# MLP up projection: GpSimd's subtractions, sums and low parts given to VectorE

## The chip, the core and the metric

The kernel runs on one core of one Trainium2 chip. The metric is the device time of one execution in microseconds. A core has five engines that work side by side, each through its own queue in order: TensorE (PE in the profile, with PEld for its weight loads), VectorE (DVE), ScalarE (ACT), GpSimd (POOL) and SyncE (SP), which here issues the DMA transfers.

## What is computed

A bidirectional encoder of two layers over 1024 tokens of width 1024, in float32. Layer 0 mixes tokens by attention, layer 1 by a gated delta rule, and each layer ends with the same gated MLP, of which this case changes the first half:

```python
D_MODEL = 1024; SEQ = 1024; D_FF = 2816; FFN_CONV = 3

def conv_ffn(h, w_up, conv_w, conv_b, w_down):
    u = depthwise_conv_centred(h @ w_up, conv_w, conv_b)
    a, b = jnp.split(u, 2, axis=-1)
    return (jax.nn.silu(a) * b) @ w_down

for i in range(DEPTH):
    y = rmsnorm(h, norm_mix[i])
    h = h + mixer(i, y)          # attention or gated delta rule, with its out projection
    h = h + conv_ffn(rmsnorm(h, norm_ffn[i]), ffn_w_up[i], ffn_conv_w[i], ffn_conv_b[i], ffn_w_down[i])
return rmsnorm(h, norm_final)
```

## The kernel before

**Split operands.** A float32 matrix is written as a high part and a low part. `split` (L108 to L110) has ScalarE cast x to the high part (L109), and another engine subtract that from x for the low part (L110): VectorE, unless the caller names an engine. `dense` (L126, its matmul is L134) then multiplies high by high, high by low and low by high, so that one 128x128 block of weights against 512 tokens takes three matmuls.

**Seven products for eight.** The up projection works on `f` from 0 to 21, each f being 128 columns of a and 128 of b. The tokens form two halves of 512 and the inner width two halves of 512, and a scheme of Strassen's kind computes the 2x2 block product with seven products p1 to p7 of 12 matmuls each, 84 in an f. TensorE takes them in the order p1, p2, p6, p5, p7, p3, p4. The weight operands are the four loaded blocks a11 to a22 and four sums `s` of them (L982, in `operands`); the token operands are named "11", "21", "t1" to "t4" and "22", and are made once in each layer by `tokens` (L893). In the trace the operands t1, t2, t3 have tiles t10h to t33l (k from 0 to 3, h high, l low), and "t4" and "22" lie in tiles called base.

**The transition.** `tokens` makes these operands while the out projection of the mixer still runs and the first f starts. The tokens come in three parts: 0:512, 512:768, 768:1024. For each part VectorE and GpSimd work out the scale 1/rms: VectorE takes mean and epsilon (L152), GpSimd the power (L153), TensorE spreads the result over the lanes (L166), and VectorE multiplies it into h (L190). Then come differences of h (L903) and their splits. Within `tokens` every third difference or low part is GpSimd's, by a counter. `start` computes p1 and p2 of f 0 and 1 before the last part is scaled; the other products of these two f wait for the last part's operands.

**The steady loop.** In each f from 2 on, VectorE makes low parts (L110) of the weight operands into tiles wl, of which three are held; two of the sums s; the first sum ua (L964), which adds p2 in tile mm to p1 and frees the accumulator that p5 of the same f writes; two further adds (L1002); four steps of the width-3 convolution (L1033 and L1035, for ua and then ub, after ScalarE has begun each at L1032); and the product with the gate (L1039). GpSimd makes the low parts of p6 and p4 and the first and third of the sums s. At each odd f, `take` of the down projection (L1057) makes four differences of the gated activations of this f and the one before (L1061, GpSimd, one of them in place in the even f's tile) and stores each by a DMA on SyncE's queue (L1060).

**The start of the down projection.** Behind the stores of the last pair, SyncE's queue holds the loads of stored activations (L1088, into raw) and of down weights (L1095).

The order of each engine's queue is fixed when the program is built, by priorities: code under `ahead(n)` is moved forward of what is written before it.

Of the kernel before, what the change touches and what calls it, by code (L numbers as in the profile page):

```python
# [13 lines left out]
ALU = mybir.AluOpType  # L14
# [862 lines left out]
class UpProjection:  # L877
# [15 lines left out]
    def tokens(self, gain):  # L893

        t, nc, h = self.t, self.nc, self.t.h
        n = [0]

        def engine():
            n[0] += 1
            return nc.vector if n[0] % 3 else nc.gpsimd  # L900

        def sub(x, z, out):
            engine().tensor_tensor(out=out, in0=x, in1=z, op=ALU.subtract)  # L903

        def put(name, k, xs, x):
            hi, lo = self.b[name][k]
            t.split(x, hi[:, xs], lo[:, xs], engine())

        with t.ahead(1):
            acc = t.big()  # L910
            bc = t.scales(HALVES[0], *(acc[:, b] for b in HALVES))
        for k in range(KT):
            x = h[k][:, HALVES[0]]
            t.scaled(x, x, gain[:, k:k + 1], bc)
            put("11" if k < 4 else "21", k % 4, slice(0, H2), x)
        ys = []
        for part, cs in enumerate(PARTS[1:]):
            xs = slice(cs.start - H2, cs.stop - H2)
            y = [[h[k][:, xs], h[k][:, cs]] for k in range(KT)]
            ys.append((xs, y))  # L920
            acc = t.bank() if part else t.big()
            with t.ahead(2):
                bc = t.scales(cs, acc[:, :2 * P], acc[:, H2 - 2 * P:H2] if part else acc[:, H2:H2 + 2 * P])
            if part == 1:
                with t.ahead(1):
                    self.start(2)
            for k in range(4):
                t.scaled(y[k][1], y[k][1], gain[:, k:k + 1], bc)
                sub(y[k][1], y[k][0], y[k][0])
                put("t1", k, xs, y[k][0])  # L930
            for k in range(4):
                t.scaled(y[k + 4][1], y[k + 4][1], gain[:, k + 4:k + 5], bc)
                sub(y[k + 4][1], y[k][0], y[k][0])
                put("t2", k, xs, y[k][0])
        for xs, y in ys:
            for k in range(4):
                sub(y[k + 4][1], y[k][1], y[k][1])
                put("t3", k, xs, y[k][1])
            for k in range(4):
                sub(y[k + 4][0], y[k][0], y[k + 4][0])  # L940
                put("t4", k, xs, y[k + 4][0])
                put("22", k, xs, y[k + 4][1])
# [23 lines left out]
    def operands(self, f):  # L966
        nc, raw = self.nc, []
        slot = lambda n: self.up.tile([P, H2], F32, name=n, bufs=2 if n[0] == "a" else 3)
        if f < 2:
            free = [self.gp.tile([P, H2], F32, name=n) for n in (3 - f) * ("gh", "gl")]  # L970
            free = iter(free if f else free + [self.rp.tile([P, H2], F32, name="raw") for _ in range(2)])
            slot = lambda n, up=slot: next(free, None) or up(n)
        for r in range(2):
            for k in range(2):
                x = slot(f"a{r}{k}")
                nc.sync.dma_start(out=x, in_=self.src(f, r, k).rearrange("p k n -> p (k n)"))
                raw.append(x)
        a11, a12, a21, a22 = raw
        s = [slot("s") for _ in range(4)]
        for i, (x, z, op, e) in enumerate(((a21, a22, ALU.add, nc.gpsimd), (s[0], a11, ALU.subtract, nc.vector),  # L980
                                           (a11, a21, ALU.subtract, nc.gpsimd), (a12, s[1], ALU.subtract, nc.vector))):
            e.tensor_tensor(out=s[i], in0=x, in1=z, op=op)  # L982
        return {"p1": (a11, "11"), "p2": (a12, "21"), "p5": (s[0], "t1"), "p6": (s[1], "t2"), "p7": (s[2], "t3"),
                "p4": (a22, "t4"), "p3": (s[3], "22")}

    def product(self, acc, ops, name, onto=False, early=0):

        x, col = ops[name]
        hi, lo = self.t.pair(self.t.wp, "w", H2)
        with self.t.ahead(early):  # L990
            self.t.split(x, hi, lo, self.nc.gpsimd if name in ("p6", "p4") else self.nc.vector)
        w = [(hi[:, k * P:(k + 1) * P], lo[:, k * P:(k + 1) * P]) for k in range(4)]
        self.t.dense(acc, w, self.b[col], [slice(0, H2)], onto=onto)

# [50 lines left out]
class DownProjection:  # L1045
# [11 lines left out]
    def take(self, f, g, pool):  # L1057

        nc = self.nc
        put = lambda n, x: nc.sync.dma_start(out=self.gd[n][f // 2], in_=x)  # L1060
        sub = lambda out, x, z: nc.gpsimd.tensor_tensor(out=out, in0=x, in1=z, op=ALU.subtract)  # L1061
        g0, g1 = (g[:, hs] for hs in HALVES)
        if f % 2 == 0:
            put("11", g0)
            self.even = g0, g1
            return
        b11, b12 = self.even
        put("21", g0)
        put("22", g1)
        t3 = pool.tile([P, H2], F32, name="t3", bufs=1)  # L1070
        sub(b11, b12, b11)
        put("t1", b11)
        sub(t3, g1, b12)
        put("t3", t3)
        sub(b12, g1, b11)
        put("t2", b12)
        sub(g0, g0, b12)
        put("t4", g0)
# [19 lines left out]
    def run(self):  # L1098
# [45 lines left out]
        a = [x[:, hs] for x in (t.big(), t.big()) for hs in HALVES]  # L1144
        b = [t.bank() for _ in range(4)]
        acc11 = product("11", w1, a, ys=lambda p: self.ready[p] if p < G_FIRST else self.tokens("11", p))
        residuals(range(4), 0)
        for m, acc in acc11:
            add(h(m, 0), acc, h(m, 0))
        a12 = [x[:, hs] for x in [t.base(i, F32) for i in range(2, 8)] for hs in HALVES][:NP]  # L1150
        for m, acc in product("21", lambda p: weights(self.load(a12[p], 0, 1, p)), b):
            read = add(h(m, 0), acc, h(m, 0))
            done(m, 0, m == 0)
# [10 lines left out]
        for m, acc in product("t1", w5, b, after=read):  # L1164
            add(h(4 + m, 1), acc, h(4 + m, 1))
# [230 lines left out]
```

## Time and profile before

| what | value |
|---|---|
| median of three runs | 3466.25 us (3457.93 to 3467.89) |
| the profiled execution: its time | 3468.96 us |
| the profiled execution: its span | 3467.2 us |
| mean granted TensorE clock | 0.976 of full speed |
| TensorE matmul busy | 3266.1 us, 94% |
| VectorE busy | 2474.7 us, 71% |
| ScalarE busy | 1730.5 us, 50% |
| GpSimd busy | 922.6 us, 27% |

The span runs from the first to the last instruction that the profiler saw; the profiled execution's own time is 1.8 us longer. A busy share is a mean over stages that have different limits, so for this change the stages count one by one: in layer 0 the transition lies at about 623 to 696 us, the steady loop at 696 to 1090 us and the start of the down projection right behind it; in layer 1 the same three lie at about 2769 to 2842, 2842 to 3222 and 3222 to 3255 us. In the timeline view a row gives start and duration of an instruction, and in brackets how long its engine sat idle before it and what ended that. "x4" in a timeline row are four instructions told as one.

### The profile page before, as it was taken

Reading aid. Unit: us, or ns where it says so; the run is one execution under the profiler, and the core shown is the slowest. Engines: PE = TensorE matmul, PEld = TensorE weight load, DVE = VectorE, ACT = ScalarE, POOL = GpSimd, SP = SyncE. Lnnn points to the kernel's source line nnn. Section 1 sums busy time; section 2 is a strip of 40 time slices with the busy share of each in tenths; the row PEclk is TensorE's granted clock in tenths of the full one; section 3 lists DMA queues with packets and bytes.
Section 4 is the critical chain, followed back from the end, with each engine's and each line's share of the span. In section 5 each row is a group of like instructions: output and inputs, shape, how many; then the busy total and the mean of one; then the engine's idle time right before and its main releaser. Section 6 shows DMA issues by size and latency. Waiting matters only on the chain. (4 is left out here: it accounts for less than half of the span.)

```text
span 3467.2 us, 54360 instructions
## 1 busy us (share of the span) xinstructions
PE 3266.1 (94%) x19690; PEld 2627.5 (76%) x19690; DVE 2474.7 (71%) x4203; ACT 1730.5 (50%) x3218; POOL 922.6 (27%) x1111
## 2 busy tenths in 40 slices
PE   7999999899999998899999999999898989999998
PEld 6887878677777776777777777777676867777776
DVE  5325886877776865877768687776853787777695
ACT  4235664544444454466655564555532544544452
POOL 1111220444442001133232223223230144444100
PEclk9999999999999999899999999999999989999999
DMA  4331116333335533233342433324256633332743
GB/s 126 107 113 55 33 33 203 111 110 112 98 101 189 197 116 100 70 112 108 92 145 70 132 109 108 114 82 137 82 190 197 199 103 110 107 99 96 240 132 108
DMA packets 249806, 411.23 MB, mean 119 GB/s; under 512 B 25537, under 2 KB 76097, under 8 KB 249537
## 3 DMA queue, kind: packets, MB, share of 16 engines
q1 hardware_dynamic: 249536, 407.76, 37.7%
q8 instruction: 155, 2.54, 0.3%
q14 instruction: 115, 0.93, 0.1%
HBM read 294.80 MB, written 107.61 MB: 116 GB/s over the span
## 5 line engine op out<-in xcount | busy, mean ns | idle before, releaser
L134 PE MATMUL mm<-base,wh 128*128 128x512 f32 x1248 | 484.0, 415 | 6.5 <-DVE t L448 6.4
L109 ACT CAST wh<-w_raw 128x512 fp32r<-128x512 f32 x275 | 170.1, 619 | 313.9 <-PE mm L134 181.7
L110 DVE TENSOR_TENSOR wl<-w_raw,wh 128x512 fp32r<-128x512 f32 x275 | 195.1, 713 | 150.9 <-ACT wh L109 140.4
L134 PE MATMUL mm<-yh,wh 128*128 128x512 f32 x736 | 286.0, 417 | 5.3 <-ACT t L291 2.7
L134 PE MATMUL mm<-yl,wh 128*128 128x512 f32 x736 | 282.1, 412 | 1.6 <-POOL yl L110 1.0
L153 POOL TENSOR_TENSOR rs<-rs,power 128x8 f32<-128x8 f32 (+2 forms) x38 | 63.4, 1669 | 822.0 <-DVE rs L152 821.7
L134 PE MATMUL mm<-yh,wl 128*128 128x512 f32 x736 | 280.1, 409 | 1.0 <-DVE wl L110 1.0
L134 PEld LDWEIGHTS mm<-base,wh 128*128 128x128 f32 x1248 | 240.4, 193 | 45.8 <-issue 4.2
L134 PE MATMUL mm<-base,wl 128*128 128x512 f32 x624 | 256.9, 412 | 6.2 <-DVE wl L110 6.2
L705 POOL TENSOR_SCALAR kd<-c,yds 128x128 f32<-128x128 f32 x224 | 92.5, 425 | 563.8 <-PE cp L734 373.7
L109 ACT CAST wh<-a 128x512 fp32r<-128x512 f32 x164 | 101.8, 621 | 252.7 <-PE mm L134 115.3
L134 PE MATMUL sp<-base,wh 128*128 128x512 f32 (+1 forms) x672 | 211.5, 373 | 12.4 <-ACT wh L109 12.4
L109 ACT CAST wh<-s 128x512 fp32r<-128x512 f32 x212 | 131.3, 619 | 176.3 <-PE sp L134 98.2
L448 DVE SCALAR_TENSOR_TENSOR t<-mm,gdn_cw,t 128x1023 f32<-128x1023 f32 (+1 forms) x128 | 163.0, 1275 | 8.3 <-ACT t L445 7.4
L134 PEld LDWEIGHTS mm<-yl,wh 128*128 128x128 f32 x736 | 140.9, 192 | 29.0 <-POOL yl L110 2.9
L134 PEld LDWEIGHTS mm<-yh,wh 128*128 128x128 f32 x736 | 140.5, 193 | 29.5 <-ACT t L291 3.6
L134 PEld LDWEIGHTS mm<-yh,wl 128*128 128x128 f32 x736 | 140.9, 192 | 25.5 <-DVE wl L110 1.7
L134 PE MATMUL sp<-base,wl 128*128 128x512 f32 (+1 forms) x432 | 157.6, 365 | 1.4 <-DVE wl L110 0.9
L134 PEld LDWEIGHTS sp<-base,wh 128*128 128x128 f32 x672 | 127.7, 190 | 34.0 <-ACT wh L109 12.8
L110 DVE TENSOR_TENSOR wl<-s,wh 128x512 fp32r<-128x512 f32 x170 | 141.8, 835 | 13.5 <-ACT wh L109 12.9
L982 POOL TENSOR_TENSOR s<-a,a 128x512 f32<-128x512 f32 x80 | 108.4, 1355 | 159.8 <-DVE s L982 106.7
L134 PEld LDWEIGHTS mm<-base,wl 128*128 128x128 f32 x624 | 119.5, 192 | 27.3 <-DVE wl L110 7.1
(522 smaller groups left out, 9417.8 us busy)
## 6 DMA issues: line engine op xcount, KB each, us to landing
a<-in_ffn_up_dram SPq DMA_DIRECT2D x160, 256.0 KB, 3.0
c<-pk SPq DMA_DIRECT2D x128, 320.0 KB, 3.1
w_raw<-in_gdn_in_dram SPq DMA_DIRECT2D x100, 256.0 KB, 2.9
g_t<-t SPq DMA_DIRECT2D x88, 256.0 KB, 2.0
raw<-g_t SPq DMA_DIRECT2D x88, 256.0 KB, 2.7
w_raw<-in_gdn_out_dram SPq DMA_DIRECT2D x68, 256.0 KB, 3.7
g<-t SPq DMA_DIRECT2D x66, 256.0 KB, 2.1
raw<-g SPq DMA_DIRECT2D x66, 256.0 KB, 2.9
```

Source lines behind the costliest of these rows:

```text
L109: self.nc.scalar.copy(out=hi, in_=src)
L110: (engine or self.nc.vector).tensor_tensor(out=lo, in0=src, in1=hi.bitcast(F32), op=ALU.subtract)
L134: self.nc.tensor.matmul(acc if one else acc[:, hs], lhsT=a, rhs=y[:, hs], start=(first and not onto and k + t == 0), stop=(last and k == n ...
L153: nc.gpsimd.tensor_tensor(out=r, in0=v, in1=self.power[:, :w], op=ALU.pow)
L448: nc.vector.scalar_tensor_tensor(out=o, in0=a, scalar=c[:, i:i + 1], in1=o, op0=ALU.mult, op1=ALU.add)
L705: nc.gpsimd.tensor_scalar(out=kd[:, e], in0=kn, scalar1=col(self.yds, e), scalar2=1.0, op0=ALU.mult, op1=ALU.mult)
L982: e.tensor_tensor(out=s[i], in0=x, in1=z, op=op)
```

## The change

Every place in the up projection that names GpSimd for a subtraction, a sum or a low part names VectorE instead. There are four: the differences and low parts in `tokens`, the first and third weight sum in `operands`, the low parts of p6 and p4 in `product`, and the four differences of `take`. GpSimd keeps the power in 1/rms (L153), and all its work in the two mixers. In all, 316 instructions move, 158 in each layer. No arithmetic changes, and SyncE issues the same transfers.

```diff
     def tokens(self, gain):
 
         t, nc, h = self.t, self.nc, self.t.h
-        n = [0]
-
-        def engine():
-            n[0] += 1
-            return nc.vector if n[0] % 3 else nc.gpsimd
 
         def sub(x, z, out):
-            engine().tensor_tensor(out=out, in0=x, in1=z, op=ALU.subtract)
+            nc.vector.tensor_tensor(out=out, in0=x, in1=z, op=ALU.subtract)
 
         def put(name, k, xs, x):
             hi, lo = self.b[name][k]
-            t.split(x, hi[:, xs], lo[:, xs], engine())
+            t.split(x, hi[:, xs], lo[:, xs])
...
-        for i, (x, z, op, e) in enumerate(((a21, a22, ALU.add, nc.gpsimd), (s[0], a11, ALU.subtract, nc.vector),
-                                           (a11, a21, ALU.subtract, nc.gpsimd), (a12, s[1], ALU.subtract, nc.vector))):
-            e.tensor_tensor(out=s[i], in0=x, in1=z, op=op)
+        for i, (x, z, op) in enumerate(((a21, a22, ALU.add), (s[0], a11, ALU.subtract), (a11, a21, ALU.subtract),
+                                        (a12, s[1], ALU.subtract))):
+            nc.vector.tensor_tensor(out=s[i], in0=x, in1=z, op=op)
...
-            self.t.split(x, hi, lo, self.nc.gpsimd if name in ("p6", "p4") else self.nc.vector)
+            self.t.split(x, hi, lo)
...
-        sub = lambda out, x, z: nc.gpsimd.tensor_tensor(out=out, in0=x, in1=z, op=ALU.subtract)
+        sub = lambda out, x, z: nc.vector.tensor_tensor(out=out, in0=x, in1=z, op=ALU.subtract)
```

Behind `tokens` the lines of the changed kernel have numbers that are 5 smaller: L903 becomes L898, L964 L959, L982 L977, L1033 L1028, L1035 L1030, L1039 L1034 and L1061 L1056.

**The order at three places.** The first is VectorE's queue in the steady loop, at an odd f (f is 3 here), from the first step of the convolution of ua (in tile t2) to the next f's first sum into ua. Before:

```order
L1033 SCALAR_TENSOR_TENSOR t2_7268<-ua_7147,ffn_cw_5852,t2_7268 128x1023
L1035 SCALAR_TENSOR_TENSOR t2_7268<-ua_7147,ffn_cw_5852,t2_7268 128x1023
L1033 SCALAR_TENSOR_TENSOR t1_7272<-ub_7182,ffn_cw_5852,t1_7272 128x1023
L1035 SCALAR_TENSOR_TENSOR t1_7272<-ub_7182,ffn_cw_5852,t1_7272 128x1023
L110 TENSOR_TENSOR wl_7361<-s_7297,wh_7360 128x512
L1039 TENSOR_TENSOR t2_7268<-t2_7268,t1_7272 128x1024
L982 TENSOR_TENSOR s_7300<-a01_7291,s_7298 128x512
L964 TENSOR_TENSOR ua_7307<-mm_7305,ua_7307 128x512
```

The same stretch of the changed kernel:

```order
L1028 SCALAR_TENSOR_TENSOR t2_7268<-ua_7147,ffn_cw_5852,t2_7268 128x1023
L110 TENSOR_TENSOR wl_7344<-s_7298,wh_7343 128x512
L1030 SCALAR_TENSOR_TENSOR t2_7268<-ua_7147,ffn_cw_5852,t2_7268 128x1023
L1028 SCALAR_TENSOR_TENSOR t1_7272<-ub_7182,ffn_cw_5852,t1_7272 128x1023
L1030 SCALAR_TENSOR_TENSOR t1_7272<-ub_7182,ffn_cw_5852,t1_7272 128x1023
L110 TENSOR_TENSOR wl_7361<-s_7297,wh_7360 128x512
L1034 TENSOR_TENSOR t2_7268<-t2_7268,t1_7272 128x1024
L977 TENSOR_TENSOR s_7300<-a01_7291,s_7298 128x512
L1056 TENSOR_TENSOR t3_7280<-t2_7268,t2_7118 128x512
L959 TENSOR_TENSOR ua_7307<-mm_7305,ua_7307 128x512
```

The low part of p6 (wl_7344) now stands between the first two steps, and one difference of `take` (t3) ahead of the first sum; the other two follow behind it. At an even f the low part is there and the difference is not.

The second place is GpSimd's queue in the transition of layer 0, around the power for the last part of the tokens (rs1_2_5936; base, t23l to t33l are low parts of token operands). Before:

```order
L110 TENSOR_TENSOR base5_5841<-h5_4683,base5_5841 128x256
L110 TENSOR_TENSOR base6_5842<-h6_4684,base6_5842 128x256
L110 TENSOR_TENSOR t23l_4674<-h3_4681,t23h_4673 128x256
L110 TENSOR_TENSOR t30l_5845<-h0_4678,t30h_5844 128x256
L110 TENSOR_TENSOR t33l_5851<-h3_4681,t33h_5850 128x256
L110 TENSOR_TENSOR base7_5843<-h7_4685,base7_5843 128x256
L153 TENSOR_TENSOR rs1_2_5936<-rs0_2_5935,power_73 128x2
L982 TENSOR_TENSOR raw_6129<-gh_6123,gh_6125 128x512
```

In the changed kernel (rs1_4_5860 and rs1_2_5895 are the powers of the first two parts; rs1_4_11483 and what follows it belong to layer 1's mixer):

```order
L153 TENSOR_TENSOR rs1_4_5860<-rs0_4_5859,power_73 128x4
L153 TENSOR_TENSOR rs1_2_5895<-rs0_2_5894,power_73 128x2
L153 TENSOR_TENSOR rs1_2_5936<-rs0_2_5935,power_73 128x2
L153 TENSOR_TENSOR rs1_4_11483<-rs0_4_11482,power_73 128x4
L110 TENSOR_TENSOR base1_11432<-h1_9496,base1_11432 128x512
```

Nothing stands in front of the power any more.

The third place is VectorE's queue in the same transition, up to the low part of p3's weights at f 0 (wl_6192), which is the first of these two f's products on the operand "22" (base). Before:

```order
L110 TENSOR_TENSOR base5_5841<-h5_4683,base5_5841 128x256
L110 TENSOR_TENSOR t33l_5851<-h3_4681,t33h_5850 128x256
L110 TENSOR_TENSOR base2_5838<-h6_4684,base2_5838 128x256
L110 TENSOR_TENSOR base6_5842<-h6_4684,base6_5842 128x256
L110 TENSOR_TENSOR base3_5839<-h7_4685,base3_5839 128x256
L110 TENSOR_TENSOR base7_5843<-h7_4685,base7_5843 128x256
L110 TENSOR_TENSOR wl_6192<-raw_6130,wh_6191 128x512
```

In the changed kernel:

```order
L110 TENSOR_TENSOR base0_5836<-h4_4682,base0_5836 128x256
L898 TENSOR_TENSOR h5_4683<-h5_4683,h1_4679 128x256
L110 TENSOR_TENSOR base5_5841<-h5_4683,base5_5841 128x256
L898 TENSOR_TENSOR h6_4684<-h6_4684,h2_4680 128x256
L110 TENSOR_TENSOR base1_5837<-h5_4683,base1_5837 128x256
L110 TENSOR_TENSOR base6_5842<-h6_4684,base6_5842 128x256
L110 TENSOR_TENSOR base2_5838<-h6_4684,base2_5838 128x256
L898 TENSOR_TENSOR h7_4685<-h7_4685,h3_4681 128x256
L110 TENSOR_TENSOR base7_5843<-h7_4685,base7_5843 128x256
L110 TENSOR_TENSOR wl_6192<-raw_6130,wh_6191 128x512
```

The low part of p3 now stands behind differences and low parts that were GpSimd's. From the first scaling (L190) of the last part to this row, VectorE's queue holds 40 instructions before and 69 now: 34 and 60 of them are 256 wide (8 of these are L190's in both), 6 and 9 are 512 wide. Some of them belong to the two earlier parts and have been moved back behind the last part's.

## Rows read from the trace of the kernel before

**Rows 1.** Busy time by stage: us and instructions of each engine, granted clock, DMA share.

```profile
623.00:696.00 73.00, 58.23 (x222) 43.15 (x220) 58.60 (x89) 36.94 (x73) 36.73 (x33) 0.91 0.31 95
696.00:1090.00 394.00, 392.17 (x1670) 311.38 (x1671) 303.07 (x304) 193.88 (x282) 176.21 (x117) 1.00 0.33 107
1090.00:1110.00 20.00, 17.74 (x72) 13.92 (x71) 11.83 (x15) 8.09 (x14) 4.73 (x3) 0.93 0.84 291
2769.00:2842.00 73.00, 60.10 (x223) 45.20 (x222) 59.85 (x90) 34.63 (x70) 36.51 (x32) 0.88 0.32 101
```

**Rows 2.** Groups by line on VectorE, 696 to 1090 us: total busy, mean ns of one.

```profile
L110 DVE TENSOR_TENSOR wl<-s,wh 128x512 fp32r<-128x512 f32 x59 | 53.2, 903 | 0.0
L1035 DVE SCALAR_TENSOR_TENSOR t<-ua,ffn_cw,t 128x1023 f32<-128x1023 f32 x20 | 34.7, 1735 | 0.7
L982 DVE TENSOR_TENSOR s<-s,a 128x512 f32<-128x512 f32 x19 | 32.2, 1693 | 22.7 <-POOL s L982 21.9
L1035 DVE SCALAR_TENSOR_TENSOR t<-ub,ffn_cw,t 128x1023 f32<-128x1023 f32 x20 | 25.7, 1284 | 0.7
L982 DVE TENSOR_TENSOR s<-a,s 128x512 f32<-128x512 f32 x19 | 13.0, 686 | 0.0
```

**Rows 3.** Timeline of the steady loop, VectorE, GpSimd, TensorE: start us, duration us, instruction.

```profile
829.25 1.72 DVE L1033 SCALAR_TENSOR_TENSOR t<-ub,ffn_cw,t 128x1023 f32<-128x1023 f32 x1 [0.52 <-ACT t L1032]
834.55 0.68 DVE L964 TENSOR_TENSOR ua<-mm,ua 128x512 f32<-128x512 f32 x1
...
847.25 2.29 DVE L1035 SCALAR_TENSOR_TENSOR t<-ua,ffn_cw,t 128x1023 f32<-128x1023 f32 x1
854.32 0.68 DVE L964 TENSOR_TENSOR ua<-mm,ua 128x512 f32<-128x512 f32 x1
854.92 1.18 DVE L110 TENSOR_TENSOR wl<-s,wh 128x512 fp32r<-128x512 f32 x1
...
847.17 1.29 POOL L110 TENSOR_TENSOR wl<-s,wh 128x512 fp32r<-128x512 f32 x1 [5.20 <-ACT wh L109]
...
834.99 0.40 PE L134 MATMUL sp<-t23h,wl 128*128 128x512 f32 x1
835.38 0.48 PE L134 MATMUL mm<-t10h,wh 128*128 128x512 f32 x1
...
854.62 0.40 PE L134 MATMUL sp<-t23h,wl 128*128 128x512 f32 x1
855.14 0.48 PE L134 MATMUL mm<-t10h,wh 128*128 128x512 f32 x1
```

**Rows 4.** Timeline of layer 0's transition, GpSimd, VectorE, TensorE.

```profile
635.49 0.70 POOL L153 TENSOR_TENSOR rs<-rs,power 128x2 f32<-128x2 f32 x1
...
633.57 0.16 DVE L152 TENSOR_SCALAR rs<-sp 128x2 f32<-128x2 f32 x1 [0.43 <-PE sp L159]
637.50 0.87 DVE L190 SCALAR_TENSOR_TENSOR h<-h,norm_ffn,sp 128x256 f32<-128x256 f32 x2 [2.56 <-PE sp L166]
655.91 1.42 DVE L110 TENSOR_TENSOR base<-h,base 128x256 fp32r<-128x256 f32 x4
658.15 4.69 DVE L110 TENSOR_TENSOR base<-h,base 128x256 fp32r<-128x256 f32 x4
662.76 0.68 DVE L110 TENSOR_TENSOR wl<-raw,wh 128x512 fp32r<-128x512 f32 x1
...
631.13 0.50 PE L134 MATMUL mm<-210h,wh 128*128 128x512 f32 x1 [2.16 <-ACT wh L109]
...
663.49 0.76 PE L134 MATMUL mm<-base,wl 128*128 128x512 f32 x1 [3.27 <-DVE wl L110]
```

**Rows 5.** Timeline of the down projection's start, GpSimd, SyncE, TensorE.

```profile
1092.64 3.38 POOL L1061 TENSOR_TENSOR t<-t,t 128x512 f32<-128x512 f32 x2 [14.63 <-DVE t L1039]
...
1094.34 4.33 SPq L1060 DMA_DIRECT2D g_t<-t  x3
...
1105.66 0.50 PE L134 MATMUL mm<-gh,base 128*128 128x512 f32 x1 [2.26 <-ACT base L109]
```

## The prediction

> **What bounds the kernel now.** I read the busy time by stage first [rows 1]. In the steady loop of layer 0 TensorE is busy 392.17 of 394 us at full clock, one matmul in 0.235 us: nothing there can be won beyond 2 us. The transition in front of it is different: TensorE is busy 58.23 of 73 us, so 14.8 us are idle, and the granted clock is 0.91, a mean over stretches at 2.4 and 1.2 GHz. Layer 1's transition reads alike, 60.10 of 73 at 0.88, 12.9 us idle. VectorE is busy 58.60 and 59.85 us of these 73: there the wait that ends last is mostly a VectorE result. At the down projection's start TensorE is busy 17.74 of 20 us and the DMA engines 0.84 of the time. So the change is decided in three places of each layer: whether the transition gets shorter, whether the steady loop stays TensorE's with more on VectorE, and whether the last stores leave earlier.
>
> The groups by line on VectorE come next [rows 2]. Instructions of one shape have two prices. A 128x512 subtraction takes 686 ns in one group (s<-a,s) and 1693 ns on average in another (s<-s,a); a convolution step takes 1284 ns on ub and 1735 on ua. The timeline tells what the long ones share [rows 3]: the step at 847.25 lasts 2.29 us, and GpSimd's low part, from 847.17 for 1.29 us, lies over its beginning. In the transition four low parts take 1.42 us at 655.91 and four others of the same shape 4.69 us at 658.15 [rows 4]. I read it so: while GpSimd works on SBUF operands, a VectorE instruction with two of them is held up. The page "SBUF — State Buffer" of the Trainium skill (section "Who interferes with whom") says that the two engines share one port pair, an exclusive lock held for a whole instruction. By it the step at 847.25 would wait for GpSimd's end at 848.46 and then take its 1.28 us, 2.49 in all; measured are 2.29, so the trace bears it out nearly.
>
> **The steady loop.** 117 GpSimd instructions of 176.21 us [rows 1] become VectorE's. A 128x512 one takes 0.68 us there and the next begins 0.60 us after it (854.32 to 854.92 [rows 3]), so 117 x 0.60 = 70 us are added. What goes is the holding up: (903 - 686) ns x 59 + (1693 - 686) x 19 + (1735 - 1284) x 20 = 12.8 + 19.1 + 9.0 = 41 us from three groups [rows 2]. VectorE comes to 303.07 + 70 - 41 = 332 of 394 us, 84%. It fits, so what matters is where in the queue the additions lie.
>
> The one VectorE result on which TensorE runs close is the first sum ua, which p5's first matmul (mm<-t10h) waits for. Its distance from the matmul before is 0.39 us at the even f (834.99 to 835.38) and 0.52 at the odd (854.62 to 855.14) [rows 3], where 0.235 is regular: late by 0.16 and 0.29. Each matmul starts 0.14 us after the sum's end (834.55 + 0.68, 854.32 + 0.68), so the sum is what it waits for. At the even f, the order puts p6's low part ahead of the sum (+0.60), but much of it falls into the 0.52 us that VectorE waited for ScalarE at 829.25, and the 1.72 us of that instruction become 1.28: 0.60 - 0.52 - 0.44 = -0.36. The 0.16 are won. At the odd f, p6's low part and the difference t3 come ahead, and 2.29 becomes 1.28: 1.20 - 1.01 = +0.19, lost. A pair of f gives -0.16 + 0.19 = +0.03, and 20 pairs in both layers +0.6 us. I take 0. The ends are -3 us (the odd f loses nothing) and +4 (the even f wins nothing). Low parts and sums for later products have microseconds of room, since a product takes 12 x 0.235 = 2.8 us and three weight tiles are held; the removed GpSimd low parts took longer than their replacements.
>
> **The transition.** Three things change. First, the power for the last part. VectorE delivers its input at 633.57 + 0.16, and GpSimd starts at 635.49, without idle time in front: it was busy with queued low parts. L190 follows 2.01 us later, at 637.50, after VectorE had idled 2.56 us [rows 4]. With nothing ahead of the power, it starts 1.7 us earlier. Second, in front of that TensorE waits 2.16 us at 631.13 for a weight cast [rows 4], which ScalarE makes behind casts of operands that come from held-up differences. I count half of it, 1.1 us. So L190 starts 2.8 us earlier. Third, from L190 to p3's low part at f 0 VectorE now takes 25.26 us (637.50 to 662.76) for 40 instructions. Of the 69 that the order puts there, 60 are 256 wide at 1.42 / 4 = 0.355 us and 9 are 512 wide at 0.60: 21.3 + 5.4 = 26.7 us if nothing holds them up. This costs 1.4 us of the 2.8, and the low part that TensorE waited 3.27 us for (663.49) comes 1.4 us earlier. But the work that was moved behind the last part, and all that GpSimd had, is done by then, so what is left for f 0 and 1 is only their weights and convolutions, with no GpSimd instruction over it: another 3 us from sums and steps held up by 1 us each. I take -4.5 us for layer 0, and in the ratio of idle time [rows 1], 4.5 x 12.9 / 14.8 = -3.9, for layer 1: -8.4. The bounds are -20 (most of the 27.7 us idle goes) and +15 (below, third rival).
>
> **The down projection's start.** SyncE's three stores take from 1094.34 on 4.33 us, as each waits for a GpSimd difference; two of these take 3.38 us from 1092.64 [rows 5]. On VectorE they take 1.3 us, so the loads queued behind can be issued some 2 us earlier, and TensorE's wait of 2.26 us (1105.66) for a weight loaded there can shrink. With the DMA engines at 0.84 [rows 1] I count half, -1 us in each layer, -2 in all; the ends are 0 and -4.6.
>
> **Sum.** -8.4 + 0 - 2 = -10.4 us. Against the profiled execution's own time that is 3468.96 - 10.4 = 3458.6. Its own time stands 2.7 us above the median, so 3466.25 - 10.4 = 3456 is the forecast.
>
> **The rivals.** *The transition stays as long.* The first operand of f 0 comes earlier, but low parts that are deferred behind the last part make TensorE wait once more, and a fresh wait brings a stretch at 1.2 GHz. What speaks for it: VectorE was busy 80% of the 73 us and its total stays about the same. Then only the down projection's 2 us are left, with a steady loss of 1: 3465.
>
> *Much more of the idle time goes.* Most waits of the transition fall on results in the chains that GpSimd or the holding up lengthen. If two thirds of the 27.7 us idle go (18.5) and the starts give 2: 3446. Against it speaks that VectorE's own instructions there remain.
>
> *VectorE's deferred block makes it slower.* The mechanism is p3's low part at f 0, behind 69 instructions instead of 40. It decides if L190 does not come earlier by more than the block grows. If L190 gains nothing and steps do not overlap as well as in the row of 1.42 (a 256-wide instruction at half of 1.42, as in the 4.69 us of the held-up row, only for the 26 added ones: 26 x 0.71 = 18.5 instead of 9.2), p3 comes 1.4 + 9.2 = 10.6 us late; the 3 us behind it come back, which leaves 7.6 a layer, 15 in both: with no gain elsewhere 3481. Against it: with GpSimd silent there is nothing in the trace that slows these rows. A rule that points this way stands in the page "Perfetto Trace Analysis" of the Trainium skill (section "Optimizing Scalar/DVE Operations"): from a VectorE that is saturated, work may rightly be offloaded, even to GpSimd, though that might not help since the two share a port. The transition is the place where VectorE is near that; by the rule's first half the change would end as this rival does, 3481, by its second as the forecast.
>
> *The long instructions have another cause than GpSimd.* Then VectorE in the steady loop comes to 373 of 394 us and the first sum is 1 us later at odd f: slower by 20 us or more. The overlap at 847.17 speaks against it.
>
> **How the numbers follow.** Forecast 3456: 0.47. Transition as long, 3465: 0.20. Much more idle gone, 3446: 0.18. Deferred block, 3481: 0.11. Another cause: 0.04. The forecast's own bounds are 3450 to 3462 (transition 0 to -14, steady +4, store side). The range leaves out the two slow cases and the far end of the big gain: 3442 to 3472. A measurement of this kernel can tell about 0.3%, 10.4 us, from no change; that is where the forecast lies, so half of its 0.47 counts as faster, with all of the big gain: 0.42. Within 0.3%: the other half and the case of 3465, 0.43. Slower: 0.15.
>
> **What would show it.** In the profile after: no VectorE group of 128x512 above about 0.7 us in the steady loop, and steps on ua at 1.28; VectorE at 84 to 87% there, with TensorE unchanged within 2 us of its 392; the distance to mm<-t10h back to 0.235 at even f and 0.7 at odd; GpSimd's power directly behind L152 and L190's idle time under 1 us; TensorE idle in each 73 us transition down by 4 to 5 us, with p5 of f 2 that much earlier; the three stores in under 3 us. It is wrong if VectorE's rows stay long, if p3's low part at f 0 comes later than 25 us after L190 by more than 3, or if p5 waits at both parities.

## The result and the profile after

The changed kernel takes 3443.08 us (median of 6 runs, 3433.94 to 3447.00) against 3464.48 us before (6 runs): the ratio is 0.994, interval 0.9926 to 0.9953, so it is 21 us faster. The forecast was 10 us faster. The profiled execution is the fastest of the six and stands 35 us below the one of before; 12 of these lie between 1190 and 2723 us, in the gated delta rule, where no line and no order changed: TensorE ran 113 us of it at half clock and was idle for 112 before, 102 and 104 after. So stages are compared, not spans. The profile of weights only below is a second one, since in its first the granted clock was 0.744.

The busy time by stage, after (columns as in [rows 1]; the transition of layer 0 now ends at 690 us, that of layer 1 lies at 2749 to 2813 us):

```profile
624.00:690.00 66.00, 55.13 (x220) 40.17 (x219) 60.23 (x124) 36.28 (x72) 0.81 (x1) 0.95 0.32 104
690.00:1081.00 391.00, 388.25 (x1671) 312.69 (x1671) 320.88 (x421) 196.06 (x283) 0.00 (x0) 1.00 0.33 108
1081.00:1101.00 20.00, 18.92 (x82) 15.04 (x82) 12.50 (x20) 8.53 (x14) 0.00 (x0) 1.00 0.91 312
2749.00:2813.00 64.00, 55.06 (x216) 40.31 (x217) 59.57 (x122) 35.32 (x69) 0.81 (x1) 0.95 0.33 107
```

With about the same matmuls (222 and 223 before, 220 and 216 after), the transitions take 66 and 64 us where they took 73, and VectorE is busy there as long as before, 60 us, with 124 instructions in place of 89 in layer 0. In the steady loop it does 421 instructions in 320.88 us, before 304 in 303.07. The groups by line say why 117 more cost so little:

```profile
L110 DVE TENSOR_TENSOR wl<-s,wh 128x512 fp32r<-128x512 f32 x78 | 53.5, 686 | 0.6 <-ACT wh L109 0.6
L1030 DVE SCALAR_TENSOR_TENSOR t<-ua,ffn_cw,t 128x1023 f32<-128x1023 f32 x20 | 25.6, 1279 | 0.0
L977 DVE TENSOR_TENSOR s<-s,a 128x512 f32<-128x512 f32 x19 | 13.1, 688 | 0.3
```

78 low parts of s take as long in all (53.5 us) as 59 did [rows 2]; the long instructions are gone, at 0.686 and 1.28 us each.

To see where the 21 us lie I matched the 19,690 matmuls of two traces one by one, by their place in the order of time, and took how far the shift between them grows over a stage (the bounds in before's time, us; minus is faster). "Transition" includes the 46 us of out projection in front of it and the first f or two behind it. The experiments below are in the same table, with the time of each against before from its own runs.

| kernel | transition 0, 577–735 | steady 0, 735–1090 | transition 1, 2723–2883 | steady 1, 2883–3222 | ratio to before (interval) |
|---|---|---|---|---|---|
| the change | -7.0 | -3.2 | -9.3 | -3.4 | 0.994 (0.9926–0.9953) |
| tokens only | +0.3 | 0.0 | +2.5 | 0.0 | 1.0013 (1.0005–1.0022) |
| weights only | -3.8 | -7.2 | -7.3 | -6.8 | 0.9921 (0.9906–0.9936) |
| take only | -1.0 | +4.6 | -3.4 | +4.0 | 1.001 (1.000–1.002) |
| all but take | -6.5 | -7.0 | -7.6 | -6.8 | 0.9914 (0.9901–0.9926) |
| change, t3 first | -1.7 | -3.2 | -4.8 | -3.3 | 0.9958 (0.9942–0.9975) |
| change, take late | -6.9 | -7.1 | -9.2 | -6.8 | 0.991 (0.9893–0.9927) |
| p4's low part only | -0.8 | -0.6 | -2.7 | -0.5 | 0.9989 (0.9978–1.000) |
| change, GpSimd reads too | +3.0 | +14.4 | +0.5 | +13.0 | 1.0096 (1.0076–1.0116) |
| change, GpSimd writes too | -7.0 | -3.2 | -9.6 | -3.4 | 0.993 (0.9915–0.9945) |

So the change won 16.3 us in the two transitions and 6.6 in the two steady loops. At the two starts of the down projection (1090 to 1110 and 3222 to 3255 us of before) it won 2.5 and 0.9, but in layer 0 it lost 3.6 again some 40 us later, at a wait of 1.99 us for h (the row at 1139.02 below) and the half clock behind it. Weights only and all but take, whose differences in `take` stay on GpSimd, lose 4.3 and 1.9 at the same place; this was not followed further.

**What the shift in the transitions is made of.** The same matmuls take less time in two ways: TensorE waits less, or it spends less of its work at half clock (1.2 GHz), where the next matmul starts 0.43 us after one and not 0.235. The busy time over the same matmuls in both layers, before and then after, tells the two apart:

```profile
577.60:735.00 157.40, 141.26 (x751) 118.01 (x752) 134.40 (x204) 83.75 (x156) 64.63 (x53) 0.96 0.43 132
2723.30:2883.20 159.90, 146.06 (x760) 122.30 (x761) 137.53 (x206) 83.36 (x157) 64.96 (x54) 0.94 0.42 132
```

```profile
579.00:729.40 150.40, 138.19 (x751) 115.28 (x752) 137.21 (x255) 84.91 (x156) 1.90 (x2) 0.98 0.43 138
2703.60:2854.20 150.60, 140.83 (x760) 117.28 (x761) 139.57 (x259) 85.93 (x157) 1.90 (x2) 0.98 0.44 142
```

In the next table idle is the length less the busy time, and the time at half clock is added up from the granted clock of the trace (all in us, one execution of each kernel).

| kernel | transition 0: busy, idle, at half clock | transition 1: busy, idle, at half clock |
|---|---|---|
| before | 141.3, 16.1, 13.7 | 146.1, 13.8, 20.5 |
| the change | 138.2, 12.2, 6.8 | 140.8, 9.8, 6.8 |
| tokens only | 140.8, 16.9, 10.2 | 145.6, 16.8, 20.5 |
| weights only | 142.7, 10.9, 17.1 | 142.9, 9.6, 17.1 |
| take only | 141.2, 15.3, 10.2 | 141.6, 14.9, 6.8 |
| all but take | 138.9, 12.0, 6.8 | 141.0, 11.3, 6.8 |
| change, t3 first | 143.4, 12.3, 17.1 | 141.7, 13.4, 10.2 |

Of the 16.3 us, 8.0 are idle time and 8.3 busy time, which fell as the time at half clock went from 34.2 us to 13.6.

**The steady loop after.** TensorE around p5's first matmul, at an even f and at an odd one, and VectorE's rows ahead of the odd one:

```profile
789.32 0.40 PE L134 MATMUL sp<-t23h,wl 128*128 128x512 f32 x1
789.55 0.39 PE L134 MATMUL mm<-t10h,wh 128*128 128x512 f32 x1
...
808.73 0.40 PE L134 MATMUL sp<-t23h,wl 128*128 128x512 f32 x1
809.33 0.47 PE L134 MATMUL mm<-t10h,wh 128*128 128x512 f32 x1 [0.20 <-DVE ua L959]
```

```profile
800.04 1.28 DVE L1028 SCALAR_TENSOR_TENSOR t<-ua,ffn_cw,t 128x1023 f32<-128x1023 f32 x1 [0.71 <-ACT t L1027]
801.24 0.69 DVE L110 TENSOR_TENSOR wl<-s,wh 128x512 fp32r<-128x512 f32 x1
801.84 1.28 DVE L1030 SCALAR_TENSOR_TENSOR t<-ua,ffn_cw,t 128x1023 f32<-128x1023 f32 x1
...
807.90 0.68 DVE L1056 TENSOR_TENSOR t<-t,t 128x512 f32<-128x512 f32 x1
808.50 0.68 DVE L959 TENSOR_TENSOR ua<-mm,ua 128x512 f32<-128x512 f32 x1
```

At the even f the distance is 0.23 us, nothing is lost; at the odd f it is 0.60 where it was 0.52 [rows 3]. The difference t3 (807.90) is the last thing ahead of the first sum, as the order said.

**The transition after.** GpSimd, VectorE and TensorE in layer 0:

```profile
631.27 0.81 POOL L153 TENSOR_TENSOR rs<-rs,power 128x2 f32<-128x2 f32 x1 [27.46 <-DVE rs L152]
...
631.04 0.16 DVE L152 TENSOR_SCALAR rs<-sp 128x2 f32<-128x2 f32 x1 [0.39 <-PE sp L159]
632.88 0.48 DVE L190 SCALAR_TENSOR_TENSOR h<-h,norm_ffn,sp 128x256 f32<-128x256 f32 x1 [0.69 <-PE sp L166]
659.57 0.69 DVE L110 TENSOR_TENSOR wl<-raw,wh 128x512 fp32r<-128x512 f32 x1
...
654.10 0.80 PE L134 MATMUL sp<-t30h,wh 128*128 128x512 f32 x1 [5.18 <-ACT t30h L109]
656.12 0.63 PE L134 MATMUL sp<-t31l,wh 128*128 128x512 f32 x1
656.55 0.63 PE L134 MATMUL sp<-t31h,wl 128*128 128x512 f32 x1
...
660.29 0.50 PE L134 MATMUL mm<-base,wh 128*128 128x512 f32 x1 [1.34 <-ACT ub L1017]
```

The power starts 0.07 us after its input is there (631.04 + 0.16), where it started 1.76 after it [rows 4]; L190 waits 0.69 us in place of 2.56 and starts 4.6 us earlier. From there to p3's low part VectorE takes 26.69 us (632.88 to 659.57), where the forecast counted 26.7. In between is a wait that before had not: TensorE stands 5.18 us for t30h, and the matmuls that follow run at half clock for a while (0.43 us from 656.12 to the next).

### The profile page after: what moved, and what is told of

Read it like the earlier page. It is cut to its first block, busy times and chain, and to the rows that moved or that the text cites. A ratio compares the mean times of both kernels' runs of the same rounds, so it can differ in the third digit from the quotient of the medians.

```text
span 3432.2 us, 54178 instructions
## 1 busy us (share of the span) xinstructions
PE 3247.3 (95%) x19690; PEld 2622.6 (76%) x19690; DVE 2511.3 (73%) x4519; ACT 1738.4 (51%) x3218; POOL 476.4 (14%) x795
## 5 line engine op out<-in xcount | busy, mean ns | idle before, releaser
L153 POOL TENSOR_TENSOR rs<-rs,power 128x8 f32<-128x8 f32 (+2 forms) x38 | 63.3, 1665 | 1828.1 <-DVE rs L152 1771.2
L134 PE MATMUL sp<-base,wh 128*128 128x512 f32 (+1 forms) x672 | 211.2, 372 | 12.2 <-ACT wh L109 12.2
L134 PEld LDWEIGHTS mm<-yl,wh 128*128 128x128 f32 x736 | 141.3, 192 | 27.4 <-POOL yl L110 1.6
L134 PEld LDWEIGHTS sp<-base,wh 128*128 128x128 f32 x672 | 127.8, 190 | 34.2 <-ACT wh L109 12.6
L110 DVE TENSOR_TENSOR wl<-a,wh 128x512 fp32r<-128x512 f32 x164 | 112.7, 687 | 34.3 <-ACT wh L109 31.0
L109 ACT CAST gh<-raw 128x512 fp32r<-128x512 f32 x132 | 81.7, 619 | 105.7 <-DMA raw<-g_t 55.0
```

Of the source, the lines that this page charges most:

```text
L109: self.nc.scalar.copy(out=hi, in_=src)
L110: (engine or self.nc.vector).tensor_tensor(out=lo, in0=src, in1=hi.bitcast(F32), op=ALU.subtract)
L134: self.nc.tensor.matmul(acc if one else acc[:, hs], lhsT=a, rhs=y[:, hs], start=(first and not onto and k + t == 0), stop=(last and k == n ...
L153: nc.gpsimd.tensor_tensor(out=r, in0=v, in1=self.power[:, :w], op=ALU.pow)
```

## The experiments

**One part alone, and all but one.** The first three kernels are the kernel before with one part of the change each, the fourth the change without one:

```diff
 tokens only
-            return nc.vector if n[0] % 3 else nc.gpsimd
+            return nc.vector
 weights only: as the diff has it in operands and product
 take only
-        sub = lambda out, x, z: nc.gpsimd.tensor_tensor(out=out, in0=x, in1=z, op=ALU.subtract)
+        sub = lambda out, x, z: nc.vector.tensor_tensor(out=out, in0=x, in1=z, op=ALU.subtract)
 all but take: the first two together
```

Tokens only. 

> Only the differences and low parts in tokens go to VectorE; weight sums, the low parts of p6 and p4 and the four differences of take stay GpSimd's. If the transition's gain is the token work that no longer queues ahead of the power and no longer holds VectorE up, both transitions shorten by most of what the full change gave there (7.0 and 8.9 us, read from the shift of matching matmuls), so 5 to 8 us each, and the steady loops keep their 0.6 us of waiting for the first sum per pair of f: 10 to 15 us faster. The rival, that the transition gains from the weights' work leaving GpSimd, gives under 4 us.

Measured: 0.13% slower. My theory fell here. The early part goes as it said: from 618 us to t22's last matmul TensorE gains 7.9 us. All of it is given back: by the wait for t30h, as long as in the changed kernel, and by three waits after it, for a weight cast, for a low part that GpSimd still makes, and for a first sum:

```profile
655.84 0.80 PE L134 MATMUL sp<-t30h,wh 128*128 128x512 f32 x1 [5.48 <-ACT t30h L109]
...
666.40 0.50 PE L134 MATMUL sp<-t20h,wh 128*128 128x512 f32 x1 [2.39 <-ACT wh L109]
667.75 0.62 PE L134 MATMUL sp<-t20h,wl 128*128 128x512 f32 x1 [0.62 <-POOL wl L110]
...
699.84 0.48 PE L134 MATMUL mm<-t10h,wh 128*128 128x512 f32 x1 [2.71 <-DVE ua L964]
```

Weights only. 

> Only the first and third weight sum and the low parts of p6 and p4 go to VectorE. If what held the first sum up in the steady loop is p6's low part on GpSimd, the first sum is no longer late at either parity (the difference t3 stays GpSimd's), and if p4's low part on GpSimd was late by itself (0.18 us per even f), that goes too: up to 0.78 us per pair, 20 pairs, 12 to 16 us faster in the steady loops together, more than the full change gave there (6.5). The rival, that VectorE merely has no room for more and the additions cost what the holding up cost, gives under 4 us.

Measured: 0.79% faster, 27 us, where the whole change gave 21; the two intervals overlap. The same kernel was then profiled again, to read it by stage.

> The weights-only kernel once more, for a profile at full clock. It should show where its 27 us lie. If the token work brings nothing in the end and the weights bring the gain in the transitions, each transition is 5 to 7 us shorter and each steady loop 7 us. If the transitions gain by token work alone, they are within 2 us of before and the steady loops must show 13 us each.

The first table has the answer: 14.0 us in the steady loops, as expected, and 11.1 in the transitions, which my first theory had given to the tokens. There TensorE's wait for p3's low part, 3.27 us before [rows 4], is gone, and its idle time fell by 5.2 and 4.2 us, more than in the change.

Take only. 

> Only the four differences of take go to VectorE. By my reading t3 then stands 0.60 us ahead of the first sum at each odd f, where TensorE already waits for it, and p6's low part still holds VectorE up there: 0.6 x 20 = 12 us slower in the steady loops, less 1 to 2 us at the down projection's two starts: 8 to 12 us slower. The rival, that any instruction taken from GpSimd frees VectorE, gives 0 to 4 us faster.

Measured: 0.1% slower, 3.5 us, with an interval that reaches to no change. The steady loops lose 8.6 us and not quite 12; the transitions give 4.4 back, which I had not counted. TensorE's idle time there is the same as before (30.2 us against 29.9 in both layers), and what is shorter is the time at half clock, 17.0 us in place of 34.2. Why is open: the work of the transition is nearly that of before. TensorE's distance to p5 at the odd f is 1.12 us in place of 0.52, the 0.60 of the difference put ahead.

All but take. 

> The full change, but the four differences of take stay GpSimd's. If t3 ahead of the first sum is what the steady loop still loses (0.45 us per odd f, 9 us in 20), this is 7 to 9 us faster than the full change, less 1 to 2 us lost at the down projection's starts: some 27 us faster than before. If GpSimd's differences hold VectorE up at another place that counts, it is no faster than the full change (21 us faster than before) or slower.

Measured: 0.86% faster, 30 us: so `take` on VectorE, with t3 ahead of the first sum, cost the change 7.2 us in the steady loops (-7.0 and -6.8 against -3.2 and -3.4). The transitions win 2.2 us less than in the change.

**Is it the order within the token work?** The change, with t3 of both late parts written ahead of t4 and 22:

```diff
         for xs, y in ys:
             for k in range(4):
                 sub(y[k + 4][1], y[k][1], y[k][1])
                 put("t3", k, xs, y[k][1])
+        for xs, y in ys:
             for k in range(4):
                 sub(y[k + 4][0], y[k][0], y[k + 4][0])
```

> The full change, with the differences and low parts of t3 for both late parts written ahead of those of t4 and 22. TensorE's wait of 5.2 us for t30h in each transition should go by 2 to 4 us. If that wait is what ends last, the kernel is 4 to 8 us faster than the full change. If p3's low part behind the same number of VectorE instructions ends last, the wait moves from p7 to p3 and the time stays within 2 us of the full change.

Measured: 0.42% faster than before, so 6 us slower than the change. The wait moved from p7 to p3, as the second reading said, but the time did not stay within 2 us, since what comes behind got worse:

```profile
650.07 0.49 PE L134 MATMUL sp<-t30h,wh 128*128 128x512 f32 x1 [1.57 <-ACT t30h L109]
...
659.53 1.22 PE L134 MATMUL mm<-base,wh 128*128 128x512 f32 x2 [4.93 <-ACT ub L1018]
```

The matmuls on base start within a microsecond of where they did (660.29). The row names ScalarE's copy into ub, which frees p3's accumulator; in ScalarE's queue it stands behind casts of base that wait for VectorE's differences (in the change the last of them at 659.35, after 0.94 us idle for h). So VectorE's sum of work up to there ends last, not its order. But behind the later wait TensorE runs at half clock, and now it has work to do there. The busy time from 659 to 669 us, in this kernel and in the change:

```profile
659.00:669.00 10.00, 8.76 (x20) 6.33 (x21) 4.85 (x10) 1.83 (x4) 0.00 (x0) 0.50 0.60 206
```

```profile
659.00:669.00 10.00, 8.26 (x34) 6.34 (x35) 9.77 (x16) 4.38 (x7) 0.00 (x0) 1.00 0.64 211
```

20 matmuls at a granted clock of 0.50 in place of 34 at 1.00, 14 of 0.235 us each, so 3.3 us. In the change the stretch at half clock lies from 651.1 to 657.9, half of it in the wait itself. In layer 0 half clock is all of the loss: 17.1 us in place of 6.8 (further stretches begin at 651.8 us and, behind a wait of 1.00 us for a low part, at 692.8 us), busy time 5.2 us longer, idle time the same. In layer 1 it is not: there are 10.2 us at half clock behind a wait of 6.53 us, but the busy time is 0.9 us longer and the idle time 3.6.

**t3 behind the first sum.** The change, with `take` called one f later:

```diff
                 self.first_sum(banks, ua)
+            if f:
+                down.take(f - 1, g, up)
...
-            down.take(f, ts[0], up)
+            g = ts[0]
+            if f == NFF - 1:
+                down.take(f, g, up)
```

> The full change, with the four differences and stores of take written behind the next f's first sum, so that t3 no longer stands ahead of it on VectorE. By the queue position theory the 0.45 us that each odd f still loses go: 8 to 9 us faster than the full change, at the down projection's starts as the full change or up to 2 us worse: 28 to 31 us faster than before. If the first sum is late for another reason than t3, nothing changes against the full change.

Measured: 3428.66 us, 0.9% faster than before, 31 us, the lowest median here, though its interval overlaps those of weights only and of all but take. The steady loops win 13.9 us, 7.3 more than in the change, the transitions stay as in the change. No distance between two matmuls in 780 to 862 us exceeds 0.25 us. TensorE is busy nearly all of the steady loop:

```profile
690.00:1078.00 388.00, 387.04 (x1676) 314.15 (x1675) 321.10 (x422) 197.25 (x285) 0.00 (x0) 1.00 0.33 110
```

**p4's low part.** The two stretches called steady in the table hold some 17.5 pairs of f, so the weights-only kernel wins 0.80 us in a pair, more than the first sum was late (0.16 + 0.29, and 0.08 behind each). In the trace of before p4's low part was late as well, at every even f, by 0.18 us over two matmuls; the forecast had given the low parts microseconds of room. GpSimd's row and TensorE's before and behind it:

```profile
822.62 1.74 POOL L110 TENSOR_TENSOR wl<-a,wh 128x512 fp32r<-128x512 f32 x1
...
823.88 0.61 PE L134 MATMUL sp<-base,wh 128*128 128x512 f32 x2
824.41 0.50 PE L134 MATMUL sp<-base,wl 128*128 128x512 f32 x1
```

The low part ends at 824.36 and the matmul on it starts at 824.41. The kernel before with p4's low part alone on VectorE:

```diff
-            self.t.split(x, hi, lo, self.nc.gpsimd if name in ("p6", "p4") else self.nc.vector)
+            self.t.split(x, hi, lo, self.nc.gpsimd if name in ("p6",) else self.nc.vector)
```

> Only p4's low part goes to VectorE, 44 instructions. If p4's low part on GpSimd is late by itself at every even f (0.18 us a pair), the steady loops gain 3 to 4 us together, and what GpSimd no longer does beside VectorE adds 0 to 2 us. If p6's low part is what matters for all of it, nothing changes (within 2 us).

Measured: 0.11% faster, 4 us, with an interval that reaches to no change; only 1.1 us lie in the steady loops, where 3 to 4 were expected. The wait for p4 is gone, but TensorE, now 0.18 us earlier, meets a first sum that is not: GpSimd's p6 low part, now at 826.41, hits the second step on ua at the even f too, and the distance to p5 there grew from 0.39 to 0.51.

```profile
826.54 2.24 DVE L1035 SCALAR_TENSOR_TENSOR t<-ua,ffn_cw,t 128x1023 f32<-128x1023 f32 x1
...
826.41 1.29 POOL L110 TENSOR_TENSOR wl<-s,wh 128x512 fp32r<-128x512 f32 x1 [4.29 <-ACT wh L109]
```

**Does GpSimd hold VectorE up, and by what?** The change, with GpSimd work beside it whose result nobody reads: in the first kernel the two sums and two subtractions that it did before, in the second a fill of the same tile after a copy of one column of the operand.

```diff
+        if f > 1:
+            scr = self.up.tile([P, H2], F32, name="scr", bufs=1)
+            self.nc.gpsimd.tensor_tensor(out=scr, in0=a21, in1=a22, op=ALU.subtract)
+            self.nc.gpsimd.tensor_tensor(out=scr, in0=a11, in1=a21, op=ALU.subtract)
...
+            if name in ("p6", "p4") and not early:
+                scr = self.up.tile([P, H2], F32, name="scr", bufs=1)
+                self.nc.gpsimd.tensor_tensor(out=scr, in0=x, in1=hi.bitcast(F32), op=ALU.subtract)
 the second kernel, at each of these places
+            self.nc.gpsimd.tensor_copy(out=scr[:, :1], in_=x[:, :1])
+            self.nc.gpsimd.memset(scr, 0.0)
```

> The full change, and beside it GpSimd subtracts the same weight operands as before (two sums and the low parts of p6 and p4 in each f) into a scratch tile that nobody reads: the work of VectorE and what it waits for are those of the full change. If GpSimd reading SBUF holds VectorE up, the groups of two SBUF operands lengthen again (a convolution step on ua to 1.7 us on average, s<-s,a over 1 us), the first sum comes up to 1 us later at odd f, and the steady loops lose 15 to 25 us. If the long instructions have another cause, they stay at 0.69 and 1.28 us and the time is that of the full change.

> The same places in the program, but GpSimd only fills the scratch tile with a constant there, after it has read one column of the operand so that it runs at the same time. If only GpSimd instructions that read whole SBUF operands hold VectorE up, its groups stay within 5% of 0.69 and 1.28 us and the time is that of the full change. If any GpSimd access does, they lengthen as in the run with reads.

Measured: with reads 0.96% slower than before, with fills 0.7% faster, as the change. VectorE's and GpSimd's groups in the kernel with reads, 700 to 1070 us:

```profile
L1037 DVE SCALAR_TENSOR_TENSOR t<-ua,ffn_cw,t 128x1023 f32<-128x1023 f32 x18 | 41.0, 2279 | 0.0
L977 DVE TENSOR_TENSOR s<-a,a 128x512 f32<-128x512 f32 x36 | 34.5, 958 | 0.0
...
L993 POOL TENSOR_TENSOR scr<-s,wh 128x512 f32<-128x512 f32 x18 | 31.8, 1769 | 57.7 <-issue 57.7
```

The same in the kernel with fills:

```profile
L1037 DVE SCALAR_TENSOR_TENSOR t<-ua,ffn_cw,t 128x1023 f32<-128x1023 f32 x19 | 24.3, 1277 | 0.0
L977 DVE TENSOR_TENSOR s<-a,a 128x512 f32<-128x512 f32 x36 | 24.6, 684 | 0.0
...
L993 POOL MEMSET scr<- 128x512 f32 x36 | 19.0, 527 | 2.1
```

Nothing waits for these GpSimd results, and yet the second step on ua takes 2.28 us in each f, 1.0 more, and the steady loops lose 34 us against the change. In before GpSimd's p6 subtraction meets that step at odd f only, here at every f; so the loss is above the 15 to 25 us expected, while the sums were held up less than expected (s<-a,a 0.96 us on average). TensorE's distance to p5 grows to 1.65 us at an odd f, from 0.60 in the change, and to 1.06 at an even one, from 0.23; 1.88 us in each of 17.5 pairs is 33:

```profile
823.87 0.40 PE L134 MATMUL sp<-t23h,wl 128*128 128x512 f32 x1
825.52 0.47 PE L134 MATMUL mm<-t10h,wh 128*128 128x512 f32 x1 [1.25 <-ACT ua L1022]
```

So the holding up is shown as a cause, at its place: GpSimd's p6 subtraction meets the step on ua, ahead of the first sum. Fills do not do it: of those in the trace many fall beside VectorE's rows (one at 813.67 for 0.53 us beside L977 at 813.49), and these stay at 0.68 or 0.69. Few fall on a convolution step, all of them in the transitions, and these steps stay at 1.28, as this one with a fill wholly inside it:

```profile
666.39 1.28 DVE L1035 SCALAR_TENSOR_TENSOR t<-ua,ffn_cw,t 128x1023 f32<-128x1023 f32 x1
...
666.56 0.53 POOL L980 MEMSET scr<- 128x512 f32 x1
```

The rule of the Trainium skill, "SBUF — State Buffer", section "SBUF: two separate sides", that VectorE instructions with two SBUF inputs meet the lock only against a GpSimd operation that reads SBUF, agrees with both runs: 2.28 us beside subtractions, 1.28 beside fills.

## Why the forecast was right in sign and half in size

*What bounds the kernel, and the cause of the long instructions:* right. VectorE's groups came out at 0.686 and 1.28 us, and the run with reads brings the long ones back. VectorE's load in the steady loop was forecast at 332 of 394 us and is 320.88 of 391: two more groups had been held up than the three of the sum, the low parts of a (0.81 us on average before) and the first step on ub (1.46).

*The steady loop, forecast 0, measured -6.6.* That nothing beyond 2 us could be won there, since TensorE is busy 392.17 of 394 us, was wrong: a matmul's record is 0.39 us long and the next one starts 0.235 us after it, so one that is late by 0.16 shows as no idle time. `take` late won 13.9 us in the two loops. The even f was right (its 0.16 us are won, and with them the 0.08 by which the next matmul starts late). At the odd f the forecast lost 0.19, and it is 0.08: p6's low part stands between two steps of which the second needs the first, and fills 0.1 us that VectorE idled there (1.20 us from start to start in place of 1.32). What was missing is p4's low part. The sentence that low parts have microseconds of room failed: in before, 0.18 us in each pair were lost on it. With 0.24 and 0.18 won and 0.08 lost a pair wins 0.34, and 17.5 pairs 6.0.

*The transition, forecast -8.4, measured -16.3.* The forecast summed idle time, and of that 3.9 and 4.1 us went, 8.0 together. What it put at nothing is the clock: [rows 1] has it at 0.91 and 0.88, but no term of the sum prices it. TensorE's busy time over the same matmuls fell by 3.1 and 5.2 us, 8.3 together, as 13.7 and 20.5 us at half clock became 6.8 and 6.8. In part this may be the one execution of before that was profiled: take only ran 10.2 and 6.8 us at half clock with nearly the same work there.

That the idle time came out is luck in part, since its terms did not. The power and the token work were given 2.8 us a layer, less 1.4 for the longer block. The earlier start was even 5.4 us in layer 0, counted from TensorE's work at 618 us, and the block was 26.7 as forecast; but of a lead of 7.7 us, counted the same, the wait for t30h takes 4.3, and tokens alone add 0.8 and 2.9 us of idle time. The weights' work, priced at 3 us a layer, takes 5.2 and 4.2 of idle time away by itself: on GpSimd a low part and two sums of these f lie over the four low parts of base that took 4.69 us [rows 4], behind which TensorE waited for p3's:

```profile
657.91 1.46 POOL L110 TENSOR_TENSOR wl<-gl,wh 128x512 fp32r<-128x512 f32 x1
659.34 1.48 POOL L982 TENSOR_TENSOR s<-gh,gl 128x512 f32<-128x512 f32 x1
660.78 1.44 POOL L982 TENSOR_TENSOR s<-gh 128x512 f32<-128x512 f32 x1
```

The change's -7.0 and -9.3 are 8.0 us more than tokens only and weights only add up to (-3.5 and -4.8). Of these, 5.7 are busy time at half clock and 2.3 idle time; no run here shows why.

*The starts of the down projection, forecast -2:* -3.4 at the starts themselves, but layer 0 did not keep its 2.5. The first two of the last stores leave in 2.11 us, the third 1.8 us later, so the three take 4.24 us and not under 3, as the third difference stands behind two other low parts on VectorE; the loads of a begin at 1090.61, in before at 1100.21 with TensorE 8.8 us later, so 0.8 us earlier; TensorE's wait for base is 1.08 us in place of 2.26:

```profile
1084.82 2.11 SPq L1055 DMA_DIRECT2D g_t<-t  x2
1088.74 0.32 SPq L1055 DMA_DIRECT2D g_t<-t  x1
1090.61 1.33 SPq L1090 DMA_DIRECT2D a<-in_ffn_down_dram  x3
...
1095.66 0.50 PE L134 MATMUL mm<-gh,base 128*128 128x512 f32 x1 [1.08 <-ACT base L109]
...
1139.02 0.63 PE L134 MATMUL sp<-gh,wh 128*128 128x512 f32 x1 [1.99 <-DVE h L1123]
```

*The rivals.* The one with much more idle time gone gave 3446 and comes nearest, 3 us off, but by luck: it needs 18.5 us of idle time gone, and 8.0 went; the rest came from the clock and from the steady loop, where it saw nothing. The one of VectorE's deferred block describes a wait that is there (t30h, 5.2 us); it did not decide, since L190 came earlier by more than the block grew. Another cause than GpSimd is ruled out by the run with reads.

## What to carry to other kernels

A helper engine that shares a path with a busy one can cost more than the work that it takes over: look for one shape with two durations in the groups by line, and for what lies beside the long ones in the timeline. Then ask of every moved instruction not whether the engine has room, but what stands behind it in the queue: here some 7 us, beside the 21 that were won, hung on one subtraction of 0.6 us in front of the one sum that TensorE waits for. Look at distances between matmuls and not at the busy share alone: a loop that was busy for 99.5% had 0.79 us in each pair of f to give. In a stage with waits, count the busy time at half clock beside the idle time. And try the parts of a change one by one, since the part that looked responsible (tokens) gave nothing by itself and the one that looked free of consequence (weight sums and low parts) gave 27 us by itself.

## What the hardware showed

The 1.0 us by which a VectorE step of 1.28 us is held up is less than the 1.29 us that a GpSimd subtraction takes alone, and the GpSimd instruction that meets VectorE's work is lengthened too, 1.77 us on average in the run with reads. A fill by GpSimd, 0.53 us of writing 128x512, is free for VectorE's two-operand instructions beside it: 0.68 us for a subtraction and 1.28 for a convolution step, as without it. Half clock stands at waits here: in the change's layer 0 it begins at 651.1 us, inside the wait of 5.18 us, and lasts to 657.9. Of the two transitions before ran 13.7 and 20.5 us at 1.2 GHz, the change 6.8 and 6.8.
